# One hybrid encoder layer on one core: attention's value transposes split in two and moved, distances of side products set per half, two weight splits moved

## Chip, core and metric

The kernel runs on one core of one Trainium2 chip. The metric is the device time of one execution in microseconds (us), the median of the runs. On the core, TensorE (PE in the profile) multiplies matrices into banks of PSUM, VectorE (DVE) and ScalarE (ACT) work on tiles, GpSimd (POOL) does a few small things, and SyncE (SP) issues most of the transfers.

## What is computed

One layer on 512 positions of 1024 channels: a norm, one wide projection `w_in`, four mixers on slices of it (short convolution a, stick-breaking attention b, RWKV-7 c, spatial gating d), a gated sum of their output projections, `w_o`, and then a gated feed-forward block with its own norm and a last norm.

```python
def hybrid_mixer(h, ...):
    proj = h @ w_in
    y_a = short_conv_mixer(proj[..., SC_OFF:SB_OFF], sc_conv_w)
    q, k, v = jnp.split(proj[..., SB_OFF:RW_OFF], 3, axis=-1)
    y_b = stick_breaking_attention(q, k, v)          # 4 heads x 64
    y_c = rwkv7_mixer(proj[..., RW_OFF:SG_OFF], ...) # 4 heads x 64
    y_d = spatial_gating(proj[..., SG_OFF:GATE_OFF], ...)
    gates = jax.nn.sigmoid(proj[..., GATE_OFF:] + gate_b)
    merged = gates[0]*(y_a @ sc_out) + gates[1]*(y_b @ sb_out) + gates[2]*(y_c @ rw_out) + gates[3]*(y_d @ sg_out)
    return merged @ w_o

# attention: A[t,s] = sig(z_ts) * prod_{s<j<t} (1 - sig(z_tj)), s < t;  out = A @ v
# RWKV-7:    S_t = S_{t-1} diag(w_t) + (S_{t-1} a_t) b_t^T + v_t k_t^T ; y_t = S_t r_t
# and a bonus: sum(r * k * r_k, over a head) * v
for l in range(DEPTH):
    h = rms_norm(x, mix_norm_g[l]);  x = x + hybrid_mixer(h, ...)
    h = rms_norm(x, ffn_norm_g[l]);  x = x + conv_glu_ffn(h, ...)
return rms_norm(x, final_norm_g)
```

## The kernel before, in words

**The main stream.** Every large product is made of two parts per operand, a high part (a cast) and a low part (the rest), and of three matmuls: high by high, high by low, low by high. That is `mm3` (L178 to L182, the matmuls are L179, L180, L181). Weights come in pieces of 128x512 through `load_piece` (the load, L125, is issued by SP) and `split` (L109: ScalarE casts `raw` to `whi`, L110, and VectorE subtracts, `wlo`, L107). There are four slots for `raw` and seven for `whi` and `wlo`, so ScalarE can run some pieces ahead of TensorE and then waits for it.

**The side threads.** The four mixers' own small products are Python generators put between the triples. Each `mm3` ends with one `tick()`, which moves every thread on; a `yield n` in a thread means that its next products stand n triples later. Thread "rw" is `rwkv_half(0)` and later `attention`, "rw1" is `rwkv_half(1)`, "sg" is `sg_tail` and later `turn_values`. Since TensorE runs in the order of the program (`manual_schedule`, L229), these numbers are TensorE's order. The orders of VectorE, ScalarE, GpSimd and SyncE are set by a scheduler, except in the first block (L292 to L333, `manual_schedule` for ScalarE and VectorE too), which runs as written.

**PSUM.** There are eight banks, four under the name `mm` for the main stream and four under `wk` for the threads. A new `wk` bank is the oldest of the four, and TensorE waits until what reads it is done.

**The places that the change touches.**
- First block: x is loaded in four tiles, x0 to x3. `mix_sums(2)` (L323) squares tile x2 on ScalarE (L240); `split(*w[2])`, `split(*w[3])` cut two pieces of the first weights; `mix_gain` (L249) makes `hf`, from which the main stream's second half of the depth for x0 and x1 is cut.
- `rwkv_half(j)`, j = 0 and 1, one half of the RWKV heads each: `ssm` (L486), then Ln and Exp on ScalarE for `y0` (L493, L494), `rk` (L501), its split into `qH` and `qL`, then `yield YA` and the products of `qH` and `qL` with ones (`head_sum`, L461). Later an inverse of blocks is made on VectorE (L576, L578), sent through DRAM (L580, L583) to `Dm` (L586); `AkV` (L605), `yield YC`, `P1` (L608) from `Dm`, `T32` and `TT`, `yield YP`, `P2`. At the end is the chain of states: six steps, each `yield YS`, one product with S (L684), two updates of S on VectorE (L685, L686), then a last `yield YS` and the output products (L693). Half 1 begins when half 0 has come to its chain.
- `sg_tail`: norm sums over the gated values (L840, L841), then L854, L855, L856 per tile on `uv`, `yield YG`, and four products from `uv` (L861).
- `attention`: per head (j, hp) three `wk` banks `zb` hold the scores (L978 to L980). ScalarE and VectorE make `az`, cut it into `spH` and `spL`, and after `yield YE` TensorE adds the suffix sums into the same banks (L999). Then `aH`, `aL`, `yield YF`, and the product with the values `vS` (L1011).
- `turn_values`: four ticks after the start, the values of both j are transposed (L955, eight matmuls into two more `wk` banks), cast (L960) and subtracted (L107) into `vS`.

Of the kernel before, what the change touches and what calls it, by code (L numbers as in the profile page):

```python
# [10 lines left out]
F32R = mybir.dt.float32r  # L11
# [4 lines left out]
P = 128  # L16
T = 512
D = 1024
NT = T // P
# [10 lines left out]
NRB, NWB = 4, 12  # L30
NACT = 8

YA, YB, YC, YD, YE, YF, YG, YH = 6, 16, 36, 20, 15, 5, 11, 3
Y1 = 3
YS = 3
YN = 5
YV = 4
YP = 5
Y0 = 8
WN = 20  # L40
WN2 = 10
# [11 lines left out]
def hybrid_encoder_layer(  # L53
# [22 lines left out]
    def bank(tag="mm"):  # L76
        return psum.tile([P, 512], F32, tag=tag, name=tag, bufs=4)
# [28 lines left out]
    def lo_of(src, hi, lo):  # L106
        vec.tensor_tensor(out=lo, in0=src, in1=hi.bitcast(F32), op=ALU.subtract)  # L107

    def split(src, hi, lo):  # L109
        act.copy(hi, src)  # L110
        lo_of(src, hi, lo)
# [126 lines left out]
    def mix_sums(tt):  # L238
        ss, sq, _ = norm_start(npool)
        act.activation(out=sq, in_=x0[tt], func=AF.Square, accum_out=ss[:, 0:1])  # L240
        return ss
# [50 lines left out]
    with tc.manual_schedule(engines={mybir.EngineType.PE, mybir.EngineType.Activation, mybir.EngineType.DVE}):  # L292
        for tt in range(2):
            mix_factor(tt, mix_sums(tt))
            dg = npool.tile([P, P], F32, tag="diag", name="diag", bufs=2)
            vec.tensor_scalar(out=dg, in0=ident, scalar1=mix_rs[tt], scalar2=None, op0=ALU.mult)
            for half in range(2):
                mix_pt[tt, half] = pt = bank()
                for k in range(4):
                    ks = slice((half * 4 + k) * P, (half * 4 + k + 1) * P)  # L300
                    pe.matmul(pt[:, k * P:(k + 1) * P], lhsT=x0[tt][:, ks], rhs=dg, start=True, stop=True)
        vec.tensor_copy(gT_mix, warm[:, P:P + KT].rearrange("p (k o) -> p k o", o=1))
        mix_xn = {}

        def mix_norm(tt, ss):
            mix_factor(tt, ss)
            mix_xn[tt] = npool.tile([P, D], F32, tag="xn", name="xn", bufs=2)
            act.mul(mix_xn[tt], x0[tt], mix_rs[tt])

        w = [raw_hi_lo for raw_hi_lo, _ in (first[0], first[1], second[0], second[1], first[2], first[3], second[2], second[3])]
        for n in range(2):
            act.copy(w[n][1], w[n][0])
        s0 = mix_gain(0, 0)
        act.copy(s0[1], s0[0])
        lo_of(*w[0])
        s1 = mix_gain(1, 0)
        act.copy(s1[1], s1[0])
        lo_of(s0[0], s0[1], s0[2])  # L320
        lo_of(s1[0], s1[1], s1[2])
        lo_of(*w[1])
        ss2 = mix_sums(2)  # L323
        split(*w[2])
        split(*w[3])
        for n in (4, 5):
            act.copy(w[n][1], w[n][0])
        s0, s1 = mix_gain(0, 1), mix_gain(1, 1)
        act.copy(s0[1], s0[0])
        act.copy(s1[1], s1[0])  # L330
        lo_of(s0[0], s0[1], s0[2])
        lo_of(s1[0], s1[1], s1[2])
        lo_of(*w[4])  # L333
        lo_of(*w[5])
        mix_norm(2, ss2)
        split(*w[6])
        split(*w[7])
        mix_norm(3, mix_sums(3))
        for raw_hi_lo, _ in third:
            split(*raw_hi_lo)  # L340
# [99 lines left out]
    def rwkv_half(j, lora, xg, zk, zr, zv):  # L440
# [59 lines left out]
        rk = t2("tI", "rk")  # L500
        vec.scalar_tensor_tensor(out=rk, in0=zr, scalar=col("r_k", j), in1=k2, op0=ALU.mult, op1=ALU.mult)  # L501
        head_sum = parts_of(rk)
        yield YA
        pb = bank("wk")
        head_sum(pb)
        t1 = t2("tI", "t1")
# [96 lines left out]

        AkV = inst("tE", "AkV")
        act.copy(AkV, all_inst(f_akv))  # L605
        yield YC
        P1 = inst("tF", "P1")
        act.copy(P1, all_inst(lambda i, hp, q, e, us: (AoT[us, i, :], Dm[us, 0, i, :])))  # L608
        yield Y1
# [2 lines left out]
        TT = inst("tI", "TT")  # L612
        vec.tensor_tensor(out=TT, in0=all_inst(lambda i, hp, q, e, us: (P1[us, i, :], Dm[us, 1, i, :])), in1=Dm[:, 1], op=ALU.add)

        yield YP

        P2 = rp.tile([P, 8, 32], F32, tag="P2", name="P2")
        p2 = bank("wk")
# [58 lines left out]

        for c in range(1, 7):
            wc = wp[:, c, 64:65]
            yield YS  # L680
            pS = bank("wk")
            for hp in range(2):
                ks = slice(64 * hp, 64 * hp + 64)
                pe.matmul(pS[ks, 0:64], lhsT=GT[ks, c, :], rhs=S[ks, c, :], start=True, stop=True)  # L684
            vec.scalar_tensor_tensor(out=S[:, c + 1, :], in0=S[:, c, :], scalar=wc, in1=S[:, c + 1, :], op0=ALU.mult, op1=ALU.add)  # L685
            vec.scalar_tensor_tensor(out=S[:, c + 1, :], in0=pS[:, 0:64], scalar=wc, in1=S[:, c + 1, :], op0=ALU.mult, op1=ALU.add)  # L686
        yield YS
        py = [bank("wk"), bank("wk")]
        for q in range(4):
            for e in range(2):  # L690
# [253 lines left out]
    vT = []  # L944
# [2 lines left out]
        act.copy(v, pss2[j])  # L947
        vT.append(v)

    def turn_values():  # L950
        yield YV
        for j in range(2):
            pt = bank("wk")
            for s in range(4):
                pe.transpose(out=pt[:, s * P:(s + 1) * P], in_=vT[j][:, s * P:(s + 1) * P], identity=ident)  # L955
            vs = apool.tile([P, 2, NT, P], F32R, tag="vS", name="vS", bufs=2)
            for hp in range(2):
                own, oth = HS[hp], HS[1 - hp]
                src = pt.rearrange("p (s c) -> p s c", s=4)[:, :, own]
                act.copy(vs[:, hp, :, own], src)  # L960
                lo_of(src, vs[:, hp, :, own], vs[:, hp, :, oth])
            vS.append(vs)

    OFF = [0, 512, 1024, 896]
    W = [512, 384, 256, 128]
    def attention():
        for j in range(2):
            yt = apool.tile([P, T], F32, tag="yt", name="yt", bufs=2)
            for hp in range(2):
                own, oth = HS[hp], HS[1 - hp]  # L970
                zb = [bank("wk"), bank("wk"), bank("wk")]

                def zreg(si, t0=0):
                    b, o = divmod(OFF[si], 512)
                    return zb[b][:, o + t0:o + W[si]]

                for si in range(4):
                    pe.matmul(zreg(si), lhsT=kS[j][:, hp, si * P:(si + 1) * P], rhs=qS[j][:, hp, si * P:T], start=(si != 3), stop=False)  # L978
                    pe.matmul(zreg(si), lhsT=kS[j][:, hp, si * P:(si + 1) * P], rhs=qL[j][:, hp, si * P:T], start=False, stop=False)
                    pe.matmul(zreg(si)[:, 0:P], lhsT=ident_r, rhs=neg_r, start=False, stop=(si != 1))  # L980
                yield Y1
                az = apool.tile([P, 1280], F32, tag="az", name="az", bufs=2)
                spH = apool.tile([P, 1280], F32R, tag="spH", name="spH", bufs=2)
                spL = apool.tile([P, 1280], F32R, tag="spL", name="spL", bufs=2)
                BR = [(0, 512, 512), (512, 1024, 512), (1024, 1280, 256)]
                for b, (a, e, w) in enumerate(BR):
                    act.activation(out=az[:, a:e], in_=zb[b][:, 0:w], func=AF.Abs)
                act.activation(out=az, in_=az, func=AF.Exp, scale=-1.0)
                act.activation(out=az, in_=az, func=AF.Ln, bias=1.0)
                for b, (a, e, w) in enumerate(BR):  # L990
                    vec.scalar_tensor_tensor(out=az[:, a:e], in0=zb[b][:, 0:w], scalar=0.0, in1=az[:, a:e], op0=ALU.max, op1=ALU.add)
                split(az, spH, spL)
                yield YE
                for si in range(4):
                    for sj in range(si, 4):
                        lt = tri_r if sj == si else mones_r
                        reg = zreg(si, (sj - si) * P)
                        for n, s_ in enumerate((spH, spL)):
                            pe.matmul(reg, lhsT=lt, rhs=s_[:, OFF[sj]:OFF[sj] + W[sj]], start=False, stop=(sj == 3 and n == 1), skip_group_check=True)  # L999
                aH = apool.tile([P, 1280], F32R, tag="spH", name="aH", bufs=2)  # L1000
                aL = apool.tile([P, 1280], F32R, tag="spL", name="aL", bufs=2)
                for b, (a, e, w) in enumerate(BR):
                    act.activation(out=az[:, a:e], in_=zb[b][:, 0:w], func=AF.Exp)
                for a, e in ((0, 512), (512, 1280)):
                    split(az[:, a:e], aH[:, a:e], aL[:, a:e])
                yield YF
                po = bank("wk")
                for si in range(4):
                    cols = slice(OFF[si], OFF[si] + W[si])
                    for n, a_ in enumerate((aH, aL)):  # L1010
                        pe.matmul(po[:, si * P:T], lhsT=vS[j][:, hp, si, :], rhs=a_[:, cols], start=(si == 0 and n == 0), stop=(si == 3 and n == 1))  # L1011
                act.copy(yt[own, :], po[oth, :])
                vec.tensor_tensor(out=yt[own, :], in0=po[own, :], in1=yt[own, :], op=ALU.add)
            y_split("b", j, yt)

    spawn("rw", attention())
    spawn("sg", turn_values())
    gates("d", False, False, range(ND, 4))
    finish("rw1")
    gates("c", False, False)  # L1020
# [182 lines left out]
```

## Time and profile before

| | us |
|---|---|
| median of 3 runs | 878.54 (878.4 to 878.56) |
| the profiled execution | 876.39 |
| its span, first to last instruction | 874.7 |
| TensorE busy | 852.4 (97%) |
| VectorE busy | 510.5 (58%) |
| ScalarE busy | 412.9 (47%) |

The profile is of one execution, 1.69 us of which lie outside its span. TensorE is busy 97% of the span; the 22.3 us in which it is not are what a reader looks for, and beside them the stretches in which it is busy at a lower granted clock, since busy time does not show these.

### The profile page before, as it was taken

The numbers are of one execution on the slowest core, as the hardware profiler recorded it, in microseconds if no ns is written. First come the engines' busy times: TensorE is split into PE (matmuls) and PEld (weight loads), VectorE is DVE, ScalarE is ACT, GpSimd is POOL, SyncE is SP. The second block draws the span as 40 slices with busy tenths as digits, with TensorE's granted clock in tenths as the row PEclk, the third lists the DMA queues.
The fourth block names the chain that finished last, engine by engine and source line by source line (L and its number), as shares of the span: only waits on it lengthen the run. The fifth ranks groups of instructions, "written<-read, shape, count | busy, mean of one in ns | idle before, by whom it ended". The sixth has DMA issues, their size and how long they took to land.

```text
span 874.7 us, 12733 instructions
## 1 busy us (share of the span) xinstructions
PE 852.4 (97%) x4815; PEld 707.0 (81%) x4815; DVE 510.5 (58%) x872; ACT 412.9 (47%) x669; POOL 11.4 (1%) x57
## 2 busy tenths in 40 slices
PE   8998999999999969999999999999999999999997
PEld 7976878788878858888888898888888888888886
DVE  5576874786447535554546576634766266644645
ACT  6483444853335648875435454423544054412425
POOL 3000100000000000000000000000000000000000
PEclk9999999999999989999999999999999999999999
DMA  7323331134223312226337253313433063311102
GB/s 249 105 61 85 103 97 50 49 88 112 76 59 86 97 36 72 58 76 210 97 96 247 72 158 96 97 49 107 135 96 97 1 194 98 98 45 60 49 1 97
DMA packets 102774, 82.21 MB, mean 94 GB/s; under 512 B 12716, under 2 KB 92152, under 8 KB 102712
## 3 DMA queue, kind: packets, MB, share of 16 engines
q1 hardware_dynamic: 102024, 79.82, 30.8%
q10 hardware_dynamic: 608, 1.32, 0.4%
q8 instruction: 38, 0.62, 0.3%
q0 software_dynamic: 80, 0.26, 0.1%
q14 instruction: 24, 0.20, 0.1%
HBM read 78.88 MB, written 2.49 MB: 93 GB/s over the span
## 4 chain that ended last, share of the span: by engine, by line
PE 92%; ACT 3%; DMA 2%; DVE 2%; issue 1%; SPq 0%; ACTq 0%
PE mm L179 25%; PE mm L181 25%; PE mm L180 25%; PE wk L181 3%; PE wk L180 3%; PE wk L179 3%; PE wk L597 1%; PE wk L999 1%; DMA raw<-in_w_down_dram 1%; DMA x<-in_x_dram 1%; PE wk L1011 1%; DMA raw<-in_w_in_dram 1%; PE wk L541 0%; PE wk L567 0%; PE wk L684 0%
## 5 line engine op out<-in xcount | busy, mean ns | idle before, releaser
L110 ACT CAST whi<-raw 128x512 fp32r<-128x512 f32 x272 | 165.9, 621 | 304.8 <-PE mm L180 179.6
L107 DVE TENSOR_TENSOR wlo<-raw,whi 128x512 fp32r<-128x512 f32 x276 | 187.4, 689 | 170.4 <-ACT whi L110 170.2
L179 PE MATMUL mm<-hH,whi 128*128 128x512 f32 (+1 forms) x432 | 167.9, 389 | 1.8 <-DVE hf L249 1.2
L180 PE MATMUL mm<-hL,whi 128*128 128x512 f32 (+1 forms) x432 | 162.7, 377 | 0.3 <-DVE hL L107 0.3
L181 PE MATMUL mm<-hH,wlo 128*128 128x512 f32 (+1 forms) x432 | 162.8, 377 | 0.0
L180 PE MATMUL mm<-h2L,whi 128*128 128x512 f32 (+1 forms) x368 | 139.9, 380 | 0.4 <-DVE h2L L107 0.4
L179 PE MATMUL mm<-h2H,whi 128*128 128x512 f32 (+1 forms) x368 | 139.9, 380 | 0.0
L181 PE MATMUL mm<-h2H,wlo 128*128 128x512 f32 (+1 forms) x368 | 139.8, 380 | 0.0
L179 PEld LDWEIGHTS mm<-hH,whi 128*128 128x128 f32 x432 | 82.2, 190 | 19.2 <-issue 1.5
L181 PEld LDWEIGHTS mm<-hH,wlo 128*128 128x128 f32 x432 | 81.8, 189 | 15.2
L180 PEld LDWEIGHTS mm<-hL,whi 128*128 128x128 f32 x432 | 82.2, 190 | 14.0 <-DVE hL L107 0.5
L180 PEld LDWEIGHTS mm<-h2L,whi 128*128 128x128 f32 x368 | 69.2, 188 | 13.8 <-DVE h2L L107 0.6
L179 PEld LDWEIGHTS mm<-h2H,whi 128*128 128x128 f32 x368 | 69.2, 188 | 13.1
L181 PEld LDWEIGHTS mm<-h2H,wlo 128*128 128x128 f32 x368 | 69.2, 188 | 13.0
L181 PE MATMUL mm<-whi,aL 128*128 128x512 f32 (+1 forms) x92 | 35.5, 386 | 0.0
L179 PE MATMUL mm<-whi,aH 128*128 128x512 f32 (+1 forms) x92 | 35.4, 385 | 0.0
L180 PE MATMUL mm<-wlo,aH 128*128 128x512 f32 (+1 forms) x92 | 35.4, 385 | 0.0
L181 PE MATMUL wk<-whi,aL 128*128 128x512 f32 (+1 forms) x88 | 33.8, 384 | 0.0
L180 PE MATMUL wk<-wlo,aH 128*128 128x512 f32 (+1 forms) x88 | 33.8, 384 | 0.0
L179 PE MATMUL wk<-whi,aH 128*128 128x512 f32 (+1 forms) x88 | 33.8, 384 | 0.0
L1110 DVE SCALAR_TENSOR_TENSOR ga<-mm,vecs,ga 128x511 f32<-128x511 f32 x22 | 16.5, 750 | 29.3 <-ACT ga L1109 29.3
L1078 DVE TENSOR_TENSOR xt<-xt,mm 128x512 f32<-128x512 f32 x16 | 11.0, 688 | 31.9 <-PE mm L181 31.9
(357 smaller groups left out, 1234.5 us busy)
## 6 DMA issues: line engine op xcount, KB each, us to landing
raw<-in_w_in_dram SPq DMA_DIRECT2D x104, 256.0 KB
raw<-in_w_up_dram SPq DMA_DIRECT2D x176, 128.0 KB
raw<-in_w_down_dram SPq DMA_DIRECT2D x44, 256.0 KB
raw<-in_w_o_dram SPq DMA_DIRECT2D x16, 256.0 KB
x<-in_x_dram SPq DMA_DIRECT2D x4, 512.0 KB
raw<-in_w_in_dram SPq DMA_DIRECT2D x16, 128.0 KB
xt<-in_x_dram SPq DMA_DIRECT2D x4, 512.0 KB
out_dram<-xn SPq DMA_DIRECT2D x4, 320.0 KB
```

The lines of the kernel that those rows point to most:

```text
L107: vec.tensor_tensor(out=lo, in0=src, in1=hi.bitcast(F32), op=ALU.subtract)
L110: act.copy(hi, src)
L179: pe.matmul(ps, lhsT=sh, rhs=mh, start=first, stop=False)
L180: pe.matmul(ps, lhsT=sh, rhs=ml, start=False, stop=False)
L181: pe.matmul(ps, lhsT=sl, rhs=mh, start=False, stop=last)
L597: pe.matmul(ps[us, i * 64:i * 64 + 64], lhsT=lt, rhs=rh, start=True, stop=True)
L999: pe.matmul(reg, lhsT=lt, rhs=s_[:, OFF[sj]:OFF[sj] + W[sj]], start=False, stop=(sj == 3 and n == 1), skip_group_check=True)
L1011: pe.matmul(po[:, si * P:T], lhsT=vS[j][:, hp, si, :], rhs=a_[:, cols], start=(si == 0 and n == 0), stop=(si == 3 and n == 1))
L1078: vec.tensor_tensor(out=xt[:, tt, half_of(hf)], in0=xt[:, tt, half_of(hf)], in1=bk, op=ALU.add)
L1110: vec.scalar_tensor_tensor(out=t0[:, 1:T], in0=ps[:, 0:T - 1], scalar=ffc(1, i), in1=t0[:, 1:T], op0=ALU.mult, op1=ALU.add)
```

## The change

- `YA`, `YC`, `YP`, `YS` become pairs, one number per half: YA 6 becomes 11 and 6, YC 36 becomes 36 and 32, YP 5 becomes 5 and 3, YS 3 becomes 3 and 2. `YG` goes from 11 to 13.
- In the first block the two splits stand ahead of `mix_sums(2)`.
- `turn_values` is no thread of its own. `attention` calls it for its own j in the first of the two heads of j, four ticks after the scores' first use (`yield YV`, YV = 4, after `yield Y1` with 3), and takes these four ticks off `YE`.

```diff
-YA, YB, YC, YD, YE, YF, YG, YH = 6, 16, 36, 20, 15, 5, 11, 3
+YB, YD, YE, YF, YG, YH = 16, 20, 15, 5, 13, 3
+
+YA, YC, YP, YS = (11, 6), (36, 32), (5, 3), (3, 2)
 Y1 = 3
-YS = 3
...
-YP = 5
...
-        ss2 = mix_sums(2)
         split(*w[2])
         split(*w[3])
+        ss2 = mix_sums(2)
...
         head_sum = parts_of(rk)
-        yield YA
+        yield YA[j]
         pb = bank("wk")
         head_sum(pb)
...
-        yield YC
+        yield YC[j]
         P1 = inst("tF", "P1")
...
-        yield YP
+        yield YP[j]
...
-            yield YS
+            yield YS[j]
             pS = bank("wk")
...
-        yield YS
+        yield YS[j]
         py = [bank("wk"), bank("wk")]
...
-    def turn_values():
-        yield YV
-        for j in range(2):
-            pt = bank("wk")
-            for s in range(4):
-                pe.transpose(out=pt[:, s * P:(s + 1) * P], in_=vT[j][:, s * P:(s + 1) * P], identity=ident)
-            vs = apool.tile([P, 2, NT, P], F32R, tag="vS", name="vS", bufs=2)
...
+    def turn_values(j):
+        pt = bank("wk")
+        for s in range(4):
+            pe.transpose(out=pt[:, s * P:(s + 1) * P], in_=vT[j][:, s * P:(s + 1) * P], identity=ident)
+        vs = apool.tile([P, 2, NT, P], F32R, tag="vS", name="vS", bufs=2)
+        for hp in range(2):
+            own, oth = HS[hp], HS[1 - hp]
+            src = pt.rearrange("p (s c) -> p s c", s=4)[:, :, own]
+            act.copy(vs[:, hp, :, own], src)
+            lo_of(src, vs[:, hp, :, own], vs[:, hp, :, oth])
+        vS.append(vs)
...
                 split(az, spH, spL)
-                yield YE
+                if hp == 0:
+                    yield YV
+                    turn_values(j)
+                yield YE - YV if hp == 0 else YE
                 for si in range(4):
...
     spawn("rw", attention())
-    spawn("sg", turn_values())
```

Three places in the engines' orders. The first is ScalarE in the first block, the order before against the order after; `hH` are parts of the normed input, `whi` casts of weights, `sq` the square of x2.

```order
 L316 CAST hH<-hf 128x4x128
 L319 CAST hH<-hf 128x4x128
+L110 CAST whi<-raw 128x512 x2
 L240 ACTIVATE sq,ss<-x_138 128x1024
-L110 CAST whi<-raw 128x512 x2
 L327 CAST whi<-raw 128x512 x2
 L329 CAST hH<-hf 128x4x128
```

The two casts stand ahead of the square instead of behind it.

The second is TensorE in the first head of the attention, before; `mm` rows are the main stream, `vT` the values, and `wk_3289`, `wk_3299` the banks of the two transposes.

```order
L179 MATMUL mm_3243<-hH_93,whi_3220 128x512
L180 MATMUL mm_3243<-hL_94,whi_3220 128x512
L181 MATMUL mm_3243<-hH_93,wlo_3221 128x512
L955 MATMUL wk_3289<-ident_88,vT_3209 128x128 x4
L955 MATMUL wk_3299<-ident_88,vT_3211 128x128 x4
L179 MATMUL mm_3243<-hH_93,whi_3220 128x512
```

The same place after; the line of the transposes is now L953.

```order
L179 MATMUL mm_3244<-hH_93,whi_3220 128x512
L180 MATMUL mm_3244<-hL_94,whi_3220 128x512
L181 MATMUL mm_3244<-hH_93,wlo_3221 128x512
L953 MATMUL wk_3298<-ident_88,vT_3209 128x128 x4
L179 MATMUL mm_3243<-hH_93,whi_3226 128x512
L180 MATMUL mm_3243<-hL_94,whi_3226 128x512
```

Only the four transposes of the first j are left here, three triples later; those of the second stand 53 triples into the attention, in the third head.

The third is VectorE in half 0's chain of states, before; L486 has just made half 1's `ssm`, L507, L508, L510 and L511 use half 1's `y0`, and the rows L685 and L686 are steps of half 0's chain.

```order
L686 SCALAR_TENSOR_TENSOR S_1765<-wk_1856,wp_833,S_1765 128x64
L685 SCALAR_TENSOR_TENSOR S_1765<-S_1765,wp_833 128x64
L526 TENSOR_TENSOR bo_1995<-wk_1900,zv_735 128x512
L686 SCALAR_TENSOR_TENSOR S_1765<-wk_1912,wp_833,S_1765 128x64
L685 SCALAR_TENSOR_TENSOR S_1765<-S_1765,wp_833 128x64
L900 TENSOR_TENSOR mg_1551<-mm_1849,gate_1847 128x512
L686 SCALAR_TENSOR_TENSOR S_1765<-wk_1926,wp_833,S_1765 128x64
L685 SCALAR_TENSOR_TENSOR S_1765<-S_1765,wp_833 128x64
L507 SCALAR_TENSOR_TENSOR t1_1903<-y0_1820,ssm_1813 128x512
L510 SCALAR_TENSOR_TENSOR kkn_1906<-zk_1538,vecs_288,y0_1820 128x512
```

The same place after, from half 1's `qL`, which follows its `ssm`; the L686 rows here are the second, third and fourth step.

```order
L107 TENSOR_TENSOR qL_1884<-rk_1881,qH_1883 128x512
L686 SCALAR_TENSOR_TENSOR S_1780<-wk_1890,wp_833,S_1780 128x64
L685 SCALAR_TENSOR_TENSOR S_1780<-S_1780,wp_833 128x64
L507 SCALAR_TENSOR_TENSOR t1_1918<-y0_1875,ssm_1868 128x512
L686 SCALAR_TENSOR_TENSOR S_1780<-wk_1904,wp_833,S_1780 128x64
L508 TENSOR_TENSOR t1_1918<-t1_1918,y0_1875 128x512
L685 SCALAR_TENSOR_TENSOR S_1780<-S_1780,wp_833 128x64
L107 TENSOR_TENSOR wlo_2043<-raw_2041,whi_2042 128x512
L510 SCALAR_TENSOR_TENSOR kkn_1921<-zk_1500,vecs_288,y0_1875 128x512
L526 TENSOR_TENSOR bo_2013<-wk_1915,zv_735 128x512
L511 SCALAR_TENSOR_TENSOR kkn_1921<-t1_1918,kkn_1921 128x512
L686 SCALAR_TENSOR_TENSOR S_1780<-wk_1927,wp_833,S_1780 128x64
```

The users of half 1's `y0` came after the fifth step before; now the first of them stands ahead of the third step and five large instructions stand between the third and the fourth.

## Rows read from the trace of the kernel before

**Rows 1.** The page: span, and busy time by engine.

```profile
span 874.7 us, 12733 instructions
PE 852.4 (97%) x4815; PEld 707.0 (81%) x4815; DVE 510.5 (58%) x872; ACT 412.9 (47%) x669; POOL 11.4 (1%) x57
```

**Rows 2.** TensorE's waits, by releaser: us in total, times, longest.

```profile
PE wk L955 <- DVE vS L107: 8.1, 1, 8.1
PE wk L461 <- ACT qH L110: 3.0, 1, 3.0
...
PE mm L179 <- DVE hf L249: 1.2, 1, 1.2
```

**Rows 3.** Stretches: us; PE, PEld, DVE, ACT, POOL busy; PEclk; DMA; GB/s.

```profile
14.60:15.90 1.30, 0.13 (x2) 0.10 (x1) 1.30 (x3) 0.90 (x3) 0.00 (x0) 1.00 1.09 351
65.40:69.10 3.70, 0.51 (x1) 0.19 (x1) 1.21 (x3) 3.67 (x7) 0.00 (x0) 1.00 0.26 71
69.10:72.50 3.40, 3.39 (x8) 2.75 (x9) 3.40 (x6) 0.27 (x1) 0.00 (x0) 0.50 0.29 77
...
251.60:266.00 14.40, 14.40 (x76) 10.44 (x76) 6.55 (x18) 3.76 (x6) 0.00 (x0) 1.00 0.27 75
306.50:314.60 8.10, 0.03 (x1) 0.06 (x2) 4.47 (x7) 4.80 (x6) 0.00 (x0) 0.80 0.12 32
314.60:318.30 3.70, 3.70 (x11) 3.12 (x12) 0.85 (x2) 0.74 (x2) 0.00 (x0) 0.51 0.00 0
```

**Rows 4.** Main stream, in time: start, us, engine, line, operation; eleven triples.

```profile
102.01 0.39 PE L179 MATMUL mm<-whi,hH 128*128 128x512 f32 x1
...
109.49 0.39 PE L179 MATMUL mm<-whi,hH 128*128 128x512 f32 x1
```

**Rows 5.** First block, in time; in brackets the idle time before, and its releaser.

```profile
1.73 4.41 SPq L125 DMA_DIRECT2D raw<-in_w_in_dram  x8
...
12.10 1.06 ACT L240 ACTIVATE sq<-x 128x1024 f32<-128x1024 f32 x1 [1.09 <-DMA x<-in_x_dram]
...
13.79 1.29 DVE L107 TENSOR_TENSOR wlo<-raw,whi 128x512 fp32r<-128x512 f32 x2 [1.46 <-ACT whi L110]
```

**Rows 6.** Half 0 of RWKV at L461, in time.

```profile
63.48 1.28 ACT L493 ACT_TABLE_LOAD   x1 [0.40 <-DVE ssm L486]
64.78 0.63 ACT L493 ACTIVATE y<-ssm 128x512 f32<-128x512 f32 x1
...
67.73 0.60 ACT L110 CAST qH<-rk 128x512 fp32r<-128x512 f32 x1
...
68.36 0.69 DVE L107 TENSOR_TENSOR qL<-rk,qH 128x512 fp32r<-128x512 f32 x1 [2.49 <-ACT qH L110]
```

**Rows 7.** First head of the attention, in time.

```profile
312.59 1.49 DVE L107 TENSOR_TENSOR spL<-az,spH 128x1280 fp32r<-128x1280 f32 x1 [1.07 <-ACT spH L110]
...
314.57 1.08 PE L955 MATMUL wk<-ident,vT 128*128 128x128 f32 x4 [8.09 <-DVE vS L107]
```

**Rows 8.** `Dm` of half 0 and the spatial gating behind it, in time.

```profile
117.10 1.29 DVE L586 TENSOR_TENSOR Dm<-Dc,dmask 128x512 f32<-128x512 f32 x2 [3.29 <-DMA Dc<-scr]
...
127.44 0.89 PE L861 MATMUL wk<-uv,wsT 128*128 128x256 f32 x3 [0.36 <-DVE uv L856]
```

**Rows 9.** Half 0's chain of states, in time.

```profile
158.26 0.69 DVE L486 TENSOR_SCALAR ssm<-wk 128x512 f32<-128x512 f32 x1
...
163.88 0.33 PE L684 MATMUL wk<-S,GT 64*64 64x64 f32 x4
...
166.40 0.33 PE L684 MATMUL wk<-S,GT 64*64 64x64 f32 x4
...
167.31 0.68 DVE L507 SCALAR_TENSOR_TENSOR t<-y,ssm 128x512 f32<-128x512 f32 x1
```

**Rows 10.** Half 1's chain of states, in time.

```profile
254.20 0.33 PE L684 MATMUL wk<-S,GT 64*64 64x64 f32 x4
...
254.69 0.28 DVE L686 SCALAR_TENSOR_TENSOR S<-wk,wp,S 128x64 f32<-128x64 f32 x1
```

More of the change, by code (lines that the diff above doesn't have):

```diff
@@ L948, in hybrid_encoder_layer @@
         vT.append(v)
-    def turn_values():
-        yield YV
-        for j in range(2):
-            pt = bank("wk")
-            for s in range(4):
-                pe.transpose(out=pt[:, s * P:(s + 1) * P], in_=vT[j][:, s * P:(s + 1) * P], identity=ident)
-            vs = apool.tile([P, 2, NT, P], F32R, tag="vS", name="vS", bufs=2)
[L957 to L962, printed above, removed]
+    def turn_values(j):
[9 more added lines that the diff above has]
+        vS.append(vs)
     OFF = [0, 512, 1024, 896]
```

## Prediction

> **What bounds the kernel now.** I read the page first: TensorE is busy 852.4 of 874.7 us [rows 1], so the end is set by its own stream, and a change can gain only where it idles (22.3 us) or runs at a lower clock. The table of its waits comes next [rows 2]: two waits stand out, 8.1 us before L955 and 3.0 us before L461, and one of 1.2 us in the first block; the rest are under 1.4 us each and the change doesn't reach them, but for 0.36 at L861 [rows 8]. Third, the stretches [rows 3]: the reader is to see the granted clock behind each long wait. After the 3 us wait it is 0.50 for 3.4 us, after the 8 us wait 0.51 for 3.7 us, so a long wait costs about half of these stretches again. The 1.2 us wait leaves the clock at 1.00 within its own stretch. Last, time lines around each place. One triple takes 0.68 us (11 triples from 102.01 to 109.49 [rows 4]); I count distances in these.
>
> **First block.** ScalarE waits 1.09 us for x2 before its square, which starts at 12.10, and the casts of w2 and w3 stand behind that; VectorE's subtraction waits 1.46 us for them, and TensorE 1.2 for `hf` behind it [rows 2, 5]. With the casts first, ScalarE starts them at 12.10 - 1.09 = 11.01 if the weights are there, and the square only moves by some tenths, since it has to wait for x2 anyway. These weights are among the eight loads issued by 6.14 [rows 5], ahead of x2 on the same queue; were they to land only with x2, the casts would still start 1.06 (the square) earlier. The subtraction can start 1.46 earlier, which is more than the wait. Gain 1.2, and not under 1.0. What comes next there (`hf`, `hL`) moves with it.
>
> **L461, half 0.** `qH` is made from 67.73 to 68.33 and `qL` from 68.36 to 69.05 [rows 6]; TensorE idles 3.19 of the 3.70 us from 65.40 on [rows 3]. Five more triples, 5 x 0.68 = 3.4, bring it to 68.8, after `qH` and 0.2 before `qL`, which the first product's own time covers for the most part: about 0.1 remains. The five triples cost nothing, they are only taken from behind the wait. The clock then has no long wait to fall at: the 3.40 us at 0.50 hold 1.7 us of full-clock work. Gain 3.19 + 1.7 - 0.1 = 4.8. If 0.5 remained it would be 4.4, and if the clock fell all the same 3.1.
>
> **L955, first head.** Three banks hold scores, one takes the first transpose, and the second transpose needs a fifth. The oldest bank is free only when the first is drained into `vS`, and those drains stand on ScalarE and VectorE behind the chain of `az`, `spH` and `spL`. After: four transposes, in the fourth bank, so nothing to wait for; the second j's transposes fall into its own first head, where they find the fourth bank likewise. The wait of 8.09 goes, and half of the 3.70 at 0.51 behind it, 1.85: 9.9.
> What is late next is `spL` itself, for the suffix sums (18 triples after the scores: 3, 4 and 11). TensorE reached the transposes at 314.57 - 8.09 = 306.48, four triples after the scores and with 0.6 of the first transposes done; 14 triples more is 316.0. `spL` ended at 312.59 + 1.49 = 314.08 [rows 7], with all of `vS` but its last piece already ahead of it. So 1.9 us are spare and no wait takes the place of this one. In the third head the two casts and two subtractions of the second `vS` are new on the way to `spL`; each covers half as many columns as the cast and the subtraction at L461, 0.60 and 0.69 [rows 6], so under 1.4 in all on either engine, again under 1.9. I take 0, and up to 0.5.
>
> **New wait at L861.** Half 0's thread is five triples later against the main stream, and the inverse behind it too. VectorE makes the two `Dm` at 117.10, after 3.29 us of waiting for the transfer, ends at 118.39, and only then turns to the norm sums of the gating; L861 starts 9.05 after that [rows 8]. After the change the order on VectorE still has both `Dm` ahead of all norm sums, with one large split (some 0.6) moved ahead of `Dm`. The main stream arrives 6.0 earlier (1.2 + 4.8), the thread 6.0 - 3.4 = 2.6 earlier. `Dm` would end at 115.8, and perhaps 1.2 sooner, since two splits fewer stand between the steps of the inverse: 114.6. Then L861 can start at 114.6 + 9.05 - 0.6 = 123.0. TensorE was there at 127.44 - 0.36 = 127.08; now 6.0 earlier, 1.4 later for two triples (`YG` 13), and 1.15 earlier for the 32 small products of `P1`, which no longer lie ahead of it: 121.3. A wait of 1.7, or 2.9 without the faster inverse, or 0.3 if `Dm` ends as early as the main stream shifts it. I take 1.3, since the queues of splits in front are also earlier: net 0.95 more than the 0.36 of before. The clock stays up, as behind the wait of 1.2 [rows 3].
>
> **New wait in half 0's chain of states.** Half 1's `ssm` ends at 158.95. From its table load to `qH` half 0 took 67.73 - 63.48 = 4.25 [rows 6], so `y0` stands at about 163.1; before, L507 used it only at 167.31 [rows 9], behind the fifth step. Now L507 stands ahead of the third step and five large instructions (0.6 to 0.7 each, 3.2 with the small update) ahead of the fourth. 163.1 + 0.6 + 0.3 (third step) + 3.2 + 0.3 puts the fourth step's end at 167.5, and the next product was wanted at 166.40: 1.1. Ends: 0 if `y0` comes 1.1 sooner, as it may since nothing stands between the two table loads now, and 2. I take 1.2 for the two steps together.
> The Trainium skill ("ScalarE: Activation LUTs", section "What ACT_TABLE_LOAD costs") puts a drain of some 1.38 us behind each load of 1.28. By it `y0` would come 2.8 later and the sum would be 2.8 longer. The rows show a load of 1.28 at 63.48 and the function at 64.78, 0.02 after its end [rows 6], and the sum goes by them.
>
> **Half 1's smaller distances.** `P1` four triples earlier and `P2` two: nothing on TensorE waits there before. The chain's steps stand two triples apart instead of three: 166.40 - 163.88 = 2.52 becomes 1.84 [rows 9]. A product at 254.20 has its update done at 254.69 + 0.28 = 254.97 [rows 10], 0.77 later, so 1.07 is left; one split of 0.7 ahead of it fits in. I take 0.1 and at most 0.5 for all seven. Fewer triples in a thread remove no triple from the stream, so they gain nothing.
>
> **Sum.** -1.2 - 4.8 - 9.9 + 0.95 + 1.2 + 0.1 = -13.65. The profiled execution is 876.39 (its span 874.7 and 1.69 around it), 2.15 under the median of 878.54. So 862.7 for such an execution, and 864.9 for the median.
>
> **Rivals.**
> 1. *No new waits.* If `Dm` and `y0` come sooner, the two new waits fall away: -15.9, 862.6. For it: both terms rest on orders and small differences; against it: VectorE's order puts the long work ahead in both places.
> 2. *A new wait grows to some 3 us and the clock falls.* A wait of 3.2 was followed by 3.4 us at 0.50 [rows 3]. One such at L861 or in half 0's chain instead of 1.2: 1.9 + 1.7 = 3.6 more, 868.5; at both 872. For it: the 2.9 worked out above; against it: the nearest row is the 1.2 that left the clock up.
> 3. *The gap returns before the suffix sums.* If `vS` and other work delay `spL` by over 1.9 us in the first or third head, the wait is back under another name: half of 9.9 would leave 869.9. Against it: the row of `spL` has most of that work ahead of it already.
> 4. *The two-triple chain drops the clock.* This one ends slower. Seven steps of half 1 with a small idle time in each could hold the clock at its lower level over the whole chain: 7 x 1.84 = 13 us of work would take 26, and the stretch behind it 3.7 more at half (1.85): 13 + 1.85 = +14.85 on the sum of -13.65, so 1.2 slower than before, 879.7. It decides against the change from 13.65 us of work at half clock. Against it: that chain at three triples ran at 1.00 with TensorE busy 14.40 of 14.40 us [rows 3], and the steps keep 1.07 of room.
> The Trainium skill ("TensorE: Matmul & The Clock Gate", section "A second HAM failure mode: psum-queue depth-cycling") describes such a going back and forth from small idle times between groups of matmuls. No row here shows it.
> 5. *The change doesn't do what it says.* The banks still meet in the attention, with the wait only moved to a new place: then only the first two terms hold, 878.5 - 6.0 + 2.2 = 874.7. Against it: the order has four transposes in each place and three banks of scores.
>
> **How the numbers follow.** Forecast (863.5 to 866.5) 0.46; rival 1 0.17; rival 2 0.22; rival 3 0.07; rival 5 0.03; rival 4 0.03; the last 0.02 for gains eaten by queues that I don't see, about no change. The predicted time is 864.9. The range reaches to rival 1 with 0.8 for errors of its terms, 861.8, and past one case of rival 2, 869.5: that leaves out some 0.17. A measurement of this kernel can tell about 0.2% (1.8 us) from no change. All but rival 4 and the last case are faster by more: faster 0.95, same 0.02, slower 0.03.
>
> **What would show it.** In the profile after: no wait of TensorE over 0.5 us at `hf`, at L461 or at the transposes (now L953); clock 1.00 around 70 and around 305 us; `uv` as releaser of some 1.3 us at the gating's products; S as releaser of about 1 us in half 0's chain, and none in half 1's. The prediction is wrong if a wait of over 3 us is left anywhere, if the clock is at half anywhere but in the first microseconds, or if TensorE's idle time doesn't fall from 22.3 to about 12.

## The result and the profile after

The changed kernel takes 863.29 us (median of 4, 862.72 to 863.62) against 878.50 (median of 4), a ratio of 0.9826 with an interval of 0.9809 to 0.9843: 15.2 us less. The forecast was 864.9, with a range of 861.8 to 869.5. Its profiled execution took 862.72 us, against 876.39 for that of before: 13.67 less, where the sum said 13.65. Why these two differences are not the same is taken up where the prediction is judged.

The page of after, span and busy time by engine:

```profile
span 861.0 us, 12724 instructions
PE 849.4 (99%) x4815; PEld 705.3 (82%) x4815; DVE 508.2 (59%) x872; ACT 409.6 (48%) x667; POOL 11.3 (1%) x57
```

Against [rows 1] TensorE's idle time falls from 22.3 to 11.6 us (861.0 - 849.4), by 10.7, and its busy time by 3.0 although it runs as many matmuls. The second is read as the work that had been done at the lower clock; half of the two stretches at 0.50 and 0.51 in [rows 3] would be 3.55. 10.7 + 3.0 is the whole 13.7. Of the 10.7, 0.7 us is not the change's doing: the wait at L301 in the first block stood at 0.9 us before,

```profile
PE mm L301 <- DVE diag L296: 0.9, 1, 0.9
```

and at 0.2 after, while other traces of kernels with the same first block as after have up to 0.8 there.

TensorE's waits of after, by releaser (us in total, times, longest), all that the view lists:

```profile
PE wk L861 <- DVE uv L856: 1.6, 1, 1.6
PE wk L684 <- DVE S L686: 1.3, 2, 0.9
PE wk L233 <- DVE ones_f L87: 1.3, 1, 1.3
PE mm L179 <- ACT hH L319: 0.5, 1, 0.5
PE mm L180 <- DVE hL L107: 0.3, 1, 0.3
PE mm L180 <- DVE h2L L107: 0.3, 1, 0.3
PE mm L301 <- DVE diag L296: 0.2, 1, 0.2
```

The three waits of [rows 2] are gone, and the first two rows are new: 1.6 us at the gating's products (0.36 before [rows 8]) and 1.3 us in half 0's chain of states (none before).

Stretches of after: us; PE, PEld, DVE, ACT, POOL busy; granted clock; DMA share; GB/s. They answer to [rows 3]: the first block, L461, the new wait at L861 and behind it, half 0's chain, half 1's chain, the first head.

```profile
14.00:16.00 2.00, 2.00 (x19) 2.00 (x18) 1.91 (x4) 1.76 (x4) 0.00 (x0) 1.00 1.07 362
64.00:68.40 4.40, 4.30 (x20) 3.25 (x19) 1.90 (x4) 4.37 (x8) 0.00 (x0) 1.00 0.22 60
68.40:72.00 3.60, 3.60 (x17) 2.99 (x16) 3.60 (x7) 1.06 (x2) 0.00 (x0) 1.00 0.47 123
121.00:122.70 1.70, 0.13 (x1) 0.03 (x1) 1.70 (x6) 0.00 (x0) 0.00 (x0) 1.00 0.00 0
122.70:126.00 3.30, 3.30 (x16) 2.56 (x16) 2.63 (x6) 0.56 (x1) 0.00 (x0) 1.00 0.47 146
152.00:170.00 18.00, 16.73 (x84) 11.64 (x84) 13.74 (x29) 11.63 (x16) 0.00 (x0) 1.00 0.18 53
243.00:257.00 14.00, 14.00 (x138) 10.10 (x133) 7.54 (x20) 2.84 (x6) 0.00 (x0) 1.00 0.20 55
307.00:313.00 6.00, 6.00 (x28) 4.91 (x27) 4.89 (x8) 5.01 (x7) 0.00 (x0) 1.00 0.21 50
```

The clock is at 1.00 in every row, where [rows 3] had 0.50 and 0.51, and TensorE is busy all the time but for 0.10 at L461, 1.57 at L861 and 1.27 in half 0's chain.

The first head of the attention, in time (start, us; what follows is the suffix sums, now L1000):

```profile
309.26 1.49 DVE L107 TENSOR_TENSOR spL<-az,spH 128x1280 fp32r<-128x1280 f32 x1 [0.48 <-ACT spH L110]
...
312.56 0.39 PE L1000 MATMUL wk<-spH,tri_r 128*128 128x512 f32 x1
```

`spL` ends at 310.75 and is wanted at 312.56: 1.8 us are spare, where the prediction had 1.9. So the 8.09 us wait is gone and not handed on.

### The profile page after: what moved, and what is told of

The parts are those of the page before. It is cut to its first block, busy times and chain, and to the rows that moved or that the text cites. A ratio compares the mean times of both kernels' runs of the same rounds, so it can differ in the third digit from the quotient of the medians.

```text
span 861.0 us, 12724 instructions
## 1 busy us (share of the span) xinstructions
PE 849.4 (99%) x4815; PEld 705.3 (82%) x4815; DVE 508.2 (59%) x872; ACT 409.6 (48%) x667; POOL 11.3 (1%) x57
## 4 chain that ended last, share of the span: by engine, by line
PE 89%; DVE 4%; DMA 2%; ACT 2%; issue 1%; SPq 0%; ACTq 0%; DVEq 0%
PE mm L179 24%; PE mm L180 23%; PE mm L181 23%; PE wk L181 3%; PE wk L180 3%; PE wk L179 3%; PE wk L597 1%; PE wk L1000 1%; DMA raw<-in_w_down_dram 1%; DVE wlo L107 1%; PE wk L1012 1%; DMA lngb<-in_sg_ln_g_dram 0%; DMA x<-in_x_dram 0%; PE wk L541 0%; PE wk L976 0%
## 5 line engine op out<-in xcount | busy, mean ns | idle before, releaser
L180 PEld LDWEIGHTS mm<-hL,whi 128*128 128x128 f32 x432 | 81.3, 188 | 13.7 <-DVE hL L107 0.5
```

The source lines that it names most:

```text
L180: pe.matmul(ps, lhsT=sh, rhs=ml, start=False, stop=False)
```

## The experiments

Times are medians, each beside runs of the kernel before on the same chip. They stood on two chips; the kernel before takes 876.75 us in the median on one and 877.15 or 877.16 on the other. The changed kernel was timed again on the first, 863.07, beside the runs with YB 11, with YG 11 and with half 1's old distances; the other runs stood on the second chip, where it was not timed. Differences to it go by 863.07 all the same, so for those a few tenths of a us show nothing. Three questions: what is each part worth, where do the two new waits come from, and when does the clock fall.

### The transposes: put back, and alone

```diff
...
-                if hp == 0:
-                    yield YV
-                    turn_values(j)
-                yield YE - YV if hp == 0 else YE
+                yield YE
...
+    spawn("sg", turn_values())
```

The first mark stands for `turn_values` itself, which is again the thread with both j in one loop.

> The changed kernel with the value transposes back in their own thread, both j at the fourth triple of the attention. Theory (the wait for a fifth bank is the cost): a wait of about 8 us at the transposes comes back, the clock is near 0.5 for some 3.7 us behind it, and the time is 9.9 to 10.4 us over the changed kernel, 873 to 874. Rival (in ordinary executions of the kernel before, which were 2.15 us over its profiled one, the stretch at the low clock behind this wait is longer): up to 12 us over, about 875. Rival (the transposes were only one of several reasons why the first head waits): 4 to 6 us.

Measured: 873.45 us, 10.4 over the changed kernel (10.2 by its first timing). The wait and the low clock behind it are back. The wait in this run, then two stretches:

```profile
PE wk L955 <- DVE vS L107: 8.1, 1, 8.1
```

```profile
304.00:312.00 8.00, 0.76 (x5) 0.79 (x5) 4.14 (x7) 4.00 (x5) 0.00 (x0) 0.78 0.13 33
312.00:316.00 4.00, 4.00 (x13) 3.21 (x12) 0.85 (x2) 1.08 (x3) 0.00 (x0) 0.58 0.00 0
```

The other way round, the kernel before with this part alone:

> The kernel before with the value transposes alone changed (four per j, inside the attention). Theory: the 8.1 us wait and the low clock behind it go, no other wait changes, and the time is 10 to 10.8 us under the kernel before on this chip, 866 to 867. Rival (the rest of the change is needed for it, since the main stream's phase matters for spL): a wait of over 0.5 us at the suffix sums, and under 9.5.

Measured: 866.72 us against 877.15, 10.4 less, and no wait at the suffix sums. The part is worth some 10.4 us with or without the rest; the theory stands, the rivals fall. Both runs move the transposes and split them by j at once. That the split does it, and not the three triples by which the first four stand later, is argued: three triples are 2.0 us, and the wait was 8.1.

### Half 0's products with ones: YA back to 6

```diff
-YA, YC, YP, YS = (11, 6), (36, 32), (5, 3), (3, 2)
+YA, YC, YP, YS = (6, 6), (36, 32), (5, 3), (3, 2)
```

> The changed kernel with six triples again ahead of half 0's products with ones. Theory: the wait of about 3 us at L461 comes back with 3.4 us at clock 0.50 behind it, +4.8 to +5.0; half 0's thread is five triples earlier, so Dm is ready before the norm sums and the wait at L861 falls from 1.6 to under 0.4, -1.2; half 0's chain against half 1's y0 stays as it is. Sum +3.6 to +3.8, about 867. Rival (the wait at L861 has nothing to do with Dm, the gating's own chain is late): 1.6 stays at L861, and +4.8 to +5.0, about 868.2.

Measured: 865.07 us (863.27 to 865.74), only 2.0 over the changed kernel; theory and rival both said more. Its two longest waits, and then three stretches around L461, explain it:

```profile
PE wk L461 <- ACT qH L110: 3.0, 1, 3.0
PE wk L233 <- DVE ones_f L87: 1.3, 1, 1.3
```

```profile
64.00:67.00 3.00, 0.29 (x2) 0.00 (x0) 0.75 (x2) 2.97 (x5) 0.00 (x0) 1.00 0.28 85
67.00:70.00 3.00, 2.50 (x10) 1.86 (x11) 2.75 (x5) 1.26 (x3) 0.00 (x0) 1.00 0.11 17
70.00:73.00 3.00, 3.00 (x15) 2.49 (x14) 3.00 (x6) 0.62 (x1) 0.00 (x0) 1.00 0.22 78
```

First, neither L861 nor L684 is among its waits: with the old distance both new waits are gone, where the theory left that in half 0's chain standing. Second, the same wait of 3.0 us stands at L461, and the clock stays at 1.00 behind it, where it fell to 0.50 in the trace of before [rows 3]. The trace of the kernel before with the transposes alone changed has that wait too, and behind it also a clock of 1.00, the wait and then the stretch behind it:

```profile
65.90:69.60 3.70, 0.53 (x2) 0.19 (x1) 1.21 (x3) 3.67 (x7) 0.00 (x0) 1.00 0.28 71
69.60:73.00 3.40, 3.36 (x15) 2.79 (x16) 3.40 (x6) 0.61 (x2) 0.00 (x0) 1.00 0.31 77
```

The four executions of this kernel took 863.27, 864.46, 865.74 and 865.67 us, with mean granted clocks over the whole program of 0.998, 0.996, 0.995 and 0.995: the shortest is the profiled one.

### The wait filled

```diff
+NFILL = 13
...
+        if j == 0:
+            for _ in range(NFILL):
+                pe.matmul(pb, lhsT=hH[:, 0, 0:P], rhs=hH[:, 0, :], start=True, stop=True)
         head_sum(pb)
```

> As the run with six triples, with 13 extra products of 128x512 (0.227 us each, 2.95 in all) written into the bank of the products with ones ahead of them, where TensorE otherwise waits; the products with ones overwrite them, so the result is the same. Theory (half of the cost is the clock that falls behind the idle time): a wait of under 0.4 at L461, clock 1.00 from 69 to 73 us, and 1.5 to 1.9 us less than the run with six triples. Rival (the clock falls there for another reason, such as the small products behind it): clock 0.50 stays and the two runs agree within 0.3.

Measured: 863.36 us (863.03 to 863.86), 1.7 under the run with six triples, with clocks of 0.998 to 1.0 in all four executions. TensorE does 13 products that nobody needs, in time in which it would have waited, and the kernel is shorter by about what the clock was to take. In the profiled pair, where the clock had not fallen, it gains next to nothing (863.03 and 863.27). The small products are still there, so the rival falls. The theory of the clock stands, with the correction that the fall doesn't come in every execution. No trace shows the fall in the kernel with six triples: it is read from the mean clocks of its slower executions (0.995 and 0.996), and L461 is its only wait over 1.3 us.

### Where the two new waits come from

YB, the distance behind the products with ones, is taken down by the five triples that YA gained, so that all of half 0's thread from there on stands where it did before:

```diff
-YB, YD, YE, YF, YG, YH = 16, 20, 15, 5, 13, 3
+YB, YD, YE, YF, YG, YH = (11, 16), 20, 15, 5, 13, 3
...
-        yield YB
+        yield YB[j]
```

> The changed kernel itself beside the others on this chip. It stands between 862.5 and 864 us on any chip if little of its time hangs on the clock (all its waits are under 1.7 us), while the kernel before, with two waits of 3 and 8 us, moves by 2 us from execution to execution with its mean granted clock.

Measured: 863.07 us (862.67 to 863.58). The kernel before lay between 874.56 and 879.88 in its nine executions beside it, with mean clocks from 0.994 to 0.989.

> The changed kernel with the distance behind half 0's products with ones (yield YB) at 11 instead of 16 for half 0, so that all of half 0's thread behind it is five triples earlier, as it was before. Theory (the waits of 1.6 us at the gating's products and of 1.3 us in half 0's chain are there because half 0's thread came five triples later): both go, nothing waits at the products of var and kbt, and the time is 2.5 to 2.9 us under the changed kernel. Rival (one of the two comes from the moved YG or from the scheduler's order for another reason): 1.2 to 1.6 us under. Rival (var and kbt aren't ready eleven triples on): a new wait of over 0.5 us there takes back part.

Measured: 859.75 us (859.55 to 860.13), 3.3 under the changed kernel, ratio to the kernel before 0.9809 (0.9786 to 0.9832). Its page and all its waits of TensorE:

```profile
PE 849.3 (99%) x4815; PEld 705.6 (82%) x4815; DVE 509.7 (59%) x872; ACT 413.4 (48%) x670; POOL 11.2 (1%) x57
```

```profile
PE wk L233 <- DVE ones_f L87: 1.3, 1, 1.3
PE mm L179 <- ACT hH L319: 0.5, 1, 0.5
PE mm L180 <- DVE hL L107: 0.3, 1, 0.3
PE mm L180 <- DVE h2L L107: 0.3, 1, 0.3
PE mm L301 <- DVE diag L296: 0.2, 1, 0.2
```

Both waits are gone and none has come in their place; no version of the study is faster by more than noise. The two waits held 2.85 us; the other 0.4 of the 3.3 is of the size by which executions of one kernel differ. Since only half 0's position against the main stream differs, that position is the cause of both. Part of how it acts at L861 the time line of VectorE in the changed kernel shows (start, us, what ended the idle time):

```profile
113.59 1.34 DVE L586 TENSOR_TENSOR Dm<-Dc,dmask 128x512 f32<-128x512 f32 x2 [3.09 <-DMA Dc<-scr]
114.85 0.74 DVE L840 BATCH_NORM_STATS2 bst<-uv 128x6 f32<-128x256 f32 x2
...
121.81 0.75 DVE L856 TENSOR_TENSOR uv<-uv,lngb 128x256 f32<-128x256 f32 x2
```

VectorE waits 3.09 us for the transfer of half 0's inverse with the norm sums queued behind, and from then on works without a gap up to `uv`; TensorE's first product from `uv` comes at 122.70:

```profile
122.70 0.45 PE L861 MATMUL wk<-uv,wsT 128*128 128x256 f32 x1 [1.58 <-DVE uv L856]
```

The other part, and the larger, is on TensorE. With YB 11 VectorE waits for the transfer no less, 3.63 us, and `uv` is done at 121.41 instead of 122.56; but TensorE reaches L861 at 124.51, where in the changed kernel it stood there from 121.12. Three groups of half 0's small products (L597: those of `P1`, `T32` and `TT`), 32 each and some 3.2 us together, stand ahead of L861 there, and none in the changed kernel (before, with YG 11, it was those of `P1` alone). The same place with YB 11:

```profile
111.56 1.29 DVE L586 TENSOR_TENSOR Dm<-Dc,dmask 128x512 f32<-128x512 f32 x2 [3.63 <-DMA Dc<-scr]
...
119.16 1.15 PE L597 MATMUL wk<-Dm,AoT 64*64 64x64 f32 x32
...
122.50 1.15 PE L597 MATMUL wk<-P,Dm 64*64 64x64 f32 x32
123.48 1.10 PE L597 MATMUL wk<-Dm,P 64*64 64x64 f32 x32
124.51 1.99 PE L861 MATMUL wk<-uv,wsT 128*128 128x256 f32 x8
```

In half 0's chain the same time line has the first user of half 1's `y0` waiting, and five large instructions ahead of the fourth step:

```profile
162.00 0.69 DVE L507 SCALAR_TENSOR_TENSOR t<-y,ssm 128x512 f32<-128x512 f32 x1 [2.87 <-ACT y L494]
162.60 0.28 DVE L686 SCALAR_TENSOR_TENSOR S<-wk,wp,S 128x64 f32<-128x64 f32 x1
...
165.46 0.68 DVE L511 SCALAR_TENSOR_TENSOR kkn<-t,kkn 128x512 f32<-128x512 f32 x1
166.06 0.28 DVE L686 SCALAR_TENSOR_TENSOR S<-wk,wp,S 128x64 f32<-128x64 f32 x1
...
166.39 0.33 PE L684 MATMUL wk<-S,GT 64*64 64x64 f32 x4 [0.86 <-DVE S L686]
```

The update of the third step waited behind L507 (0.41 on TensorE at the product after it), that of the fourth behind the next five (0.86).

### The gating's distance back to 11

```diff
-YB, YD, YE, YF, YG, YH = 16, 20, 15, 5, 13, 3
+YB, YD, YE, YF, YG, YH = 16, 20, 15, 5, 11, 3
```

> The changed kernel with 11 triples instead of 13 ahead of the gating's products. Theory (uv's end is set by VectorE, which waits for Dm): TensorE arrives 1.4 us earlier, the wait at L861 grows from 1.6 to 3.0 and the products start at the same time; the 1.4 us of main stream follow behind them, so the wait costs +1.4 us, or +2.5 to +3.1 where the clock falls behind it as it did behind the 3 us wait of before. Rival (uv moves with the main stream): the wait stays at 1.6 and the time is the same within 0.3.

Measured: 865.87 us (864.88 to 866.82), 2.8 over the changed kernel. Its wait and the stretch behind it:

```profile
PE wk L861 <- DVE uv L856: 2.8, 1, 2.8
```

```profile
123.00:126.00 3.00, 3.00 (x15) 2.53 (x14) 2.08 (x6) 0.62 (x1) 0.00 (x0) 1.00 0.31 87
```

The wait grows by 1.2 us and `uv` doesn't move (122.44 against 122.56), as the theory has it. In the profiled execution (864.88, mean clock 0.999) the clock stays up and the loss is 1.3 over the profiled execution of the changed kernel beside it (863.58); the other three took 865.79 to 866.82 with mean clocks of 0.996 and 0.997. So a wait of 2.8 us seems to behave like the one of 3.0 at L461; no trace shows the fall here either.

### The other parts

> The changed kernel with the square of x2 ahead of the two weight splits again. Theory: TensorE waits 1.2 us at hf again, and the time is 1.0 to 1.3 us over the changed kernel, 864.3 to 864.6. Rival (the next link, the casts of hf, would have been late anyway): under 0.4 us.

```diff
+        ss2 = mix_sums(2)
         split(*w[2])
         split(*w[3])
-        ss2 = mix_sums(2)
```

Measured: 864.07 us, 0.8 to 1.0 over the changed kernel in its two timings (863.29 and 863.07); the rival falls, and the wait at `hf` is back:

```profile
PE mm L179 <- DVE hf L249: 1.0, 1, 1.0
```

> The changed kernel with half 1's distances as before (36, 5, 3). Its thread, now five triples later, isn't through with its chain when the main stream reaches the point where the program pulls it to its end, so the last two steps and the output products stand one and no triple apart. The prediction on record held these distances for worth nothing: then within 0.3 us. Theory after reading the order: TensorE waits for S before the last step (about 0.3) and before the output products (about 0.8), 0.8 to 1.2 us over the changed kernel.

```diff
-YA, YC, YP, YS = (11, 6), (36, 32), (5, 3), (3, 2)
+YA, YC, YP, YS = (11, 6), (36, 36), (5, 5), (3, 3)
```

Measured: 863.76 us, 0.7 over the changed kernel, every execution (863.70 to 864.18) above all of the changed kernel's beside it. TensorE's time line in this run at the end of half 1's chain, where the steps before stood 2.5 us apart:

```profile
261.60 0.33 PE L684 MATMUL wk<-S,GT 64*64 64x64 f32 x4
262.75 0.27 PE L684 MATMUL wk<-S,GT 64*64 64x64 f32 x2
...
264.67 0.33 PE L693 MATMUL wk<-S,var 64*64 64x64 f32 x4 [1.12 <-DVE S L686]
```

The last step comes 1.15 us after the one before, the output products at once, and the last of them wait 1.12 us for S. The wait before the last step, which the theory had at 0.3, does not come. So half 1's smaller distances are worth 0.7 us, but only since half 0 was moved back. That they have no worth of their own the next run shows:

> The changed kernel with YB 11 for half 0, and half 1's distances as before (36, 5, 3). Half 1's thread then ends its chain at the triple at which it did before, and nothing is pulled. Theory (half 1's smaller distances only make room for the five triples of half 0): within 0.3 us of the run with YB 11, 859.6 to 860.1. Rival (they save something of their own): over 0.5 us more.

```diff
-YB, YD, YE, YF, YG, YH = 16, 20, 15, 5, 13, 3
+YB, YD, YE, YF, YG, YH = (11, 16), 20, 15, 5, 13, 3
-YA, YC, YP, YS = (11, 6), (36, 32), (5, 3), (3, 2)
+YA, YC, YP, YS = (11, 6), (36, 36), (5, 5), (3, 3)
...
-        yield YB
+        yield YB[j]
```

Measured: 859.79 us, against 859.75 with the smaller distances (each beside the kernel before on its chip: 0.9797 and 0.9809, within each other's intervals). The last run takes the moved products alone, in the kernel before:

> The kernel before with YA 11 and YB 11 for half 0 alone: the products with ones five triples later, all behind them where it was. Theory: the 3.2 us of waiting at L461 and, in executions in which the clock falls behind it, up to 1.7 more go, and no new wait comes: 3.2 to 4.9 us under the kernel before, 872 to 873.5. Rival (var and kbt are late with it): under 2.5.

```diff
-YA, YB, YC, YD, YE, YF, YG, YH = 6, 16, 36, 20, 15, 5, 11, 3
+YA, YB, YC, YD, YE, YF, YG, YH = (11, 6), (11, 16), 36, 20, 15, 5, 11, 3
...
-        yield YA
+        yield YA[j]
...
-        yield YB
+        yield YB[j]
```

Measured: 872.70 us against 877.15, 4.5 less, between the two prices (3.2 without the clock, 4.9 with it), and no new wait. With the parts above this makes 10.4 + 4.5 + 0.9 = 15.8 without the new waits. The two versions with YB 11 are 17.0 and 17.4 under the kernel before, each on its chip. The 1.2 to 1.6 us between are not accounted for; the kernel before varies by 4 to 5 us from execution to execution, so they may be noise.

## Why the prediction was right, and where not

- **First block.** Forecast -1.2; the wait is gone, and undoing it costs 0.8 to 1.0. Right.
- **L461.** The wait went as worked out: 0.10 is left. Its price of 4.8 took for granted that the clock falls behind it. It did in the trace of before, and not in the two other traces with the same wait (YA 6, and the transposes alone); alone, the part is worth 4.5 in the median. Mechanism right, the size right for an execution like that of before.
- **L955.** Forecast -9.9, measured some 10.4 both ways, with 1.8 us spare at the suffix sums against 1.9. Right.
- **Wait at L861.** Forecast a wait of 1.3 between 0.3 and 2.9; it is 1.58. `Dm` ends at 114.93 (worked out: 114.6), L861 starts at 122.70 (123.0). Right, and the value of 1.7 that the rows gave was nearer than the 1.3 that I took.
- **Wait in half 0's chain.** Forecast 1.2 for the two steps, measured 0.41 + 0.86 = 1.27. The mechanism is right; that the size is so near is partly luck. `y0` came 3.86 us after the end of `ssm` (158.01 to 161.87), not 4.15, but the product that waits was also wanted sooner, 7.11 us after it (166.39 - 0.86 - 0.41 = 165.12) and not 7.45, and the two errors cancel. Half 1's `y0` took 3.78 us from its table load (158.09 to 161.87) where half 0's had taken 4.25. The drain that the Trainium skill ("ScalarE: Activation LUTs", section "What ACT_TABLE_LOAD costs") puts behind a table load does not show here either; the trace decides against it. The load of 1.28 at 158.09 is followed by the function at 159.38, 0.01 after its end:

```profile
158.09 1.28 ACT L493 ACT_TABLE_LOAD   x1 [1.07 <-DVE ssm L486]
159.38 0.63 ACT L493 ACTIVATE y<-ssm 128x512 f32<-128x512 f32 x1
```

- **Half 1's smaller distances.** "Fewer triples in a thread remove no triple from the stream, so they gain nothing": this step was wrong. They remove none, but half 0's five triples push half 1's chain to the place where the program pulls it on ahead of the attention, and without the smaller distances that costs 0.7 us. I had counted them at 0.1 of loss; with them no wait is seen in half 1's chain. The error lay in not asking what the rest of the change would do to a thread whose own numbers I then priced against the trace of before.
- **The sum.** 13.65 and 13.67 are nearer than the terms are. 0.7 us at L301 belongs to no term, and TensorE's busy time fell by 3.0 where the two stretches were put at 3.55; the two nearly cancel.
- **The signs.** Waits, releasers and the idle time of 11.6 came as named. That the clock is at half in the first microseconds only fits neither trace: it is 1.00 over the first 2 us of both, and low at the end (0.60 over the last 2 us of after), when TensorE has done its last product. By its words that was a sign of being wrong, but no work of TensorE is left there to slow.
- **Rivals.** The clock did not fall in the two-triple chain (1.00 from 243 to 257 us), so the slower case had nothing in it, and what the Trainium skill ("TensorE: Matmul & The Clock Gate", section "A second HAM failure mode: psum-queue depth-cycling") describes is seen in no run here. No new wait reached 3 us; rival 2 came true only in the run with YG 11, where 2.8 us of wait cost 2.8 in the median.
- **The step from the execution to the median.** This is where the 1.6 us between 864.9 and 863.29 come from, and it is the step that was off: I added to the profiled execution the 2.15 us by which that of before stood under its median, and after, that distance is 0.57. The kernel before takes 874.56 to 879.88 us in the executions beside the second timing, mostly longer where its mean clock is lower (0.994 at 874.56, 0.989 at 879.88, but 0.994 at 877.04 too). The changed kernel has no wait after which the clock fell in any trace, and stays within 862.67 and 863.62 in the eight executions seen. So the distance can't be carried over. That it belongs to the two long waits is likely and not shown: the profiled execution of before already has the low clock behind both [rows 3], so what makes other executions of it 2 us longer stands in no trace here. In the second timing the difference of medians is 876.75 - 863.07 = 13.7, the sum's own number; since the median of before moved by 1.75 between the two timings, this too is in part chance.

What stays open is what decides, in a given execution, whether the clock falls behind a wait of 3 us, and where the slower executions of the kernel before lose their time; the runs show only that they do.

## What to carry to other kernels

A wait of TensorE is dissolved by moving the waiting products later in the stream, but everything behind them in the same thread moves too: take the same number of triples out of a later distance that has room (here YB, whose operands were ready in time: no new wait came), or waits come back elsewhere; here that cost 3.3 us. Look at both sides of such a new wait: the producer that is late, and the products that no longer stand ahead of the waiting one. A bank wait in a rotation of four was cured here by keeping to the rotation, one bank for one purpose where its reader is already done. And don't carry the distance between a profiled execution and the median over to another kernel.

## What the runs showed of the hardware

Behind an idle time of TensorE of 3 us the granted clock falls in some traces and not in others: 0.50 for 3.4 us in the trace of before [rows 3], 1.00 in the profiled runs with YA 6 and with the transposes alone, at the same place behind the same wait of 3.0. Executions of one kernel with that wait then differ by 2.5 us (863.27 to 865.74), while kernels with no wait over 1.8 us, or with the wait filled by needless products, stay within 1 us. With the wait of 8.1 us the clock was low in all three traces that have it, already within the wait (0.80, 0.78 and 0.63 over its stretch) and for some 4 us behind it (0.51 in the trace of before, 0.58 with the transposes put back, 0.50 in the last run, with the moved products alone).
